# A hybrid decoder layer: gate tiles spread among the mixer's projections, a pool of their own for the first results of each feed-forward, and later places for two kinds of transposes

## The chip, the cores and the metric

The kernel runs on one core of a Trainium2 chip. TensorE multiplies matrices, VectorE, ScalarE and GpSimd (DVE, ACT and POOL in the profile) work on tiles in the on-chip memory SBUF and on the accumulators' banks in PSUM (GpSimd on SBUF alone here), and SyncE issues most of the transfers. The metric is the time of one execution on the device in microseconds, lower is better. Each engine works through its own list of instructions in order, and waits where an instruction needs something that is not there yet.

## The reference

One layer of a decoder for two groups of requests: 1024 tokens of one prompt, and 8 sequences of 4 new tokens each with a past of 4096. Width 1024, inner width of the feed-forward 2816, all in fp32:

```python
x += 1/2 * gate1 * SwiGLU1(mod(RMSNorm(x)))
x += gate2 * W_out [GDN heads | MLA heads](mod(RMSNorm(x)))
x += 1/2 * gate3 * SwiGLU2(mod(RMSNorm(x)))

def swiglu_ffn(h, wi, wo):
    gate, up = jnp.split(h @ wi, 2, axis=-1)
    return (jax.nn.silu(gate) * up) @ wo

def causal_conv(prev, x, w):
    xin = jnp.concatenate([prev.astype(x.dtype), x], axis=1)
    y = sum(xin[:, j:j + T] * w[j] for j in range(GDN_CONV))
    return jax.nn.silu(y), xin[:, xin.shape[1] - (GDN_CONV - 1):]
```

`mod` is a shift and a scale per sequence, worked out from a conditioning vector. The mixer's input projection has 2992 columns: 1536 for the queries, keys and values of 8 gated-delta heads (a convolution over 4 tokens and SiLU run over them, queries and keys are scaled to length 1 per head), 512 for the gate `z` of their output (SiLU), 16 for two small factors, 768 for the queries of 8 latent-attention heads, 128 for the latents, and 32 for rotary keys.

## The kernel before

The 1056 tokens lie as columns in 4 blocks of 264 (1024 channels as 8 groups of 128 rows). Every fp32 product is three matmuls of a rounded format, weights high by input high, high by low, low by high (`mm3`, lines 127 to 129), so inputs and weights are first split in a high part (ScalarE) and a low part (VectorE or GpSimd; `halve`, lines 369 and 370).

Stages by the trace: the start with the conditioning and the first norm up to about 50 us; the first feed-forward's up product to 575; its down product to 860; the mixer's projections 868 to 1283; the heads to 1974; the mixer's output to 2082; the second feed-forward's up product to 2550 and its down product to the end.

**Order.** The program is written as instructions with priorities, and a scheduler lists them per engine by priority and by when it expects their inputs; `high_priority(n)` moves what stands in it ahead by n, `later(n)` back by n. GpSimd's part is listed in the order of the program.

**Mixer's projections** (`mixer_in`, line 1259). `ORDER` (line 44) names the column tiles of 128 in their order: k, q, v (convolved), m (latent queries), c (latents), z (gate), and two marks, I (the inverses of the 64 x 64 triangular blocks, 31 steps at lines 1082 and 1084, all on VectorE) and F (the finish of the latent queries, nine token tiles on lines 1106 to 1166). A tile is 4 groups of 24 matmuls into a bank `pp`, one per block. After each group `hook` lets the follow-up work of earlier tiles go one step on; that work is written as generators. A convolved tile then costs: copies out of the bank (ScalarE), one tap on ScalarE and three on VectorE (line 913), SiLU (915, 916), nine transposes back to tokens (`to_tokens`, bank `ptk`, line 701), for queries and keys the sum of squares (930) and the scaling (938) of `tok`, and the way back to channels as eight transposes (`channels`, bank `pch`, line 953), twice. Values are scaled from ptk (1050, 1053). A gate tile costs one SiLU per group, straight out of its bank (`zt`, line 1246), and a store: nothing on VectorE or GpSimd. `raw`, `cy`, `tok` and `zt` are tiles of small rings. Three groups of transposes (`pnc`, line 1336) at the end collect the new state of the convolution.

**Feed-forward up** (`ffn_up`, line 505). Per tile of 128 inner columns there are seven products of 12 matmuls (`PRODUCTS`) for each pair of blocks, into three banks X, Z, Y. `ffn_pair` reads them: `s1` copies X to SBUF (line 487), `u2`, `u3` and the halves of `cc` add banks to it on VectorE (line 476), `sg` is SiLU, and `cc` is stored. In the first and the last tile the two pairs go one after the other, else in turn. The input of a pair, tiles B and T (sums and differences of the normed blocks, split in halves), is made by VectorE and ScalarE (lines 354 to 405, 369, 370) just ahead of the first tile, per block from `rb`, the reciprocal root mean square of every token broadcast over the rows (line 347). `norm_sums` (line 326) works it out from `nacc`.

**Mixer's output** (`mixer_out`, line 2079) works through eight output tiles, the last two for blocks 2 and 3 at the end, while blocks 0 and 1 are already normed for the second feed-forward. `LATE` holds the numbers that put the small matmuls of these norms later; its fourth is the one for `rb` of block 2.

## Time and profile before

| | us |
|---|---|
| three runs | 2831.9, 2836.54, 2845.81 (median 2836.54) |
| the profiled execution | 2833.71 |
| its span on the core | 2830.8 |
| TensorE busy in the span | 2659.3 (94%) |
| VectorE busy | 1716.5 (61%) |
| ScalarE / GpSimd busy | 1082.2 / 1082.9 (38% each) |
| mean granted clock of TensorE | 0.956 |

The span is from the first to the last instruction on the core; the execution lasts 2.9 us longer. "Idle before" is the time that an engine waited ahead of an instruction, followed by what ended the wait. A matmul's end is modelled, and they overlap, so the spacing of their starts is the surer number. PEclk is the clock that was granted to TensorE, as a share of the full one.

### The profile page before, as it was taken

How to read it: one execution, taken by the hardware profiler on the slowest of the kernel's cores; microseconds unless marked ns; L12 is line 12 of the kernel's file. 1: busy time of each engine (PE TensorE's matmuls, PEld its weight loads, DVE VectorE, ACT ScalarE, POOL GpSimd, SP SyncE). 2: the span in 40 equal slices, each digit the busy share in tenths (PEclk: the TensorE clock that was granted, in tenths of full speed). 3: DMA queues.
4: the chain of work that ended last, by engine and by line, in shares of the span. 5: the costliest groups of instructions: out<-in, count | busy, mean ns of one | idle time of the engine just before them, and what ended most of it. 6: DMA issues, size and time to landing. Idle time of an engine off the chain costs nothing.

```text
span 2830.8 us, 53341 instructions
## 1 busy us (share of the span) xinstructions
PE 2659.3 (94%) x21536; PEld 2459.8 (87%) x21536; DVE 1716.5 (61%) x3315; ACT 1082.2 (38%) x2055; POOL 1082.9 (38%) x1032
## 2 busy tenths in 40 slices
PE   4899999989999898799999999998979999999999
PEld 3788989989998887788888877776979999999999
DVE  7644444555564678856766666875585554546555
ACT  5322223322134543424666665553443333331111
POOL 0222223223342555653444465671433333323331
PEclk7999999999999899898999999997979999999999
DMA  7454452243232473432112243323422222234322
GB/s 274 149 172 128 128 165 91 72 173 99 85 102 78 150 205 115 146 130 83 44 51 62 61 97 107 103 66 95 147 73 91 76 84 76 84 111 140 99 76 70
DMA packets 339489, 308.34 MB, mean 109 GB/s; under 512 B 93865, under 2 KB 282017, under 8 KB 336171
## 3 DMA queue, kind: packets, MB, share of 16 engines
q1 hardware_dynamic: 304837, 246.32, 28.5%
q10 hardware_dynamic: 28262, 37.64, 4.1%
q0 software_dynamic: 6144, 20.98, 2.3%
q8 instruction: 169, 2.77, 0.4%
q14 instruction: 77, 0.63, 0.1%
HBM read 229.29 MB, written 75.59 MB: 108 GB/s over the span
## 4 chain that ended last, share of the span: by engine, by line
PE 43%; DVE 5%; issue 3%; POOL 3%; DMA 2%; ACT 1%; POOLq 0%; DVEq 0%; ACTq 0%; SPq 0%
PE po L127 4%; PE po L128 4%; PE po L129 4%; PE pY L127 2%; PE pY L128 2%; PE pY L129 2%; PE kraw L127 2%; PE pX L127 2%; PE pX L128 2%; PE pX L129 2%; PE pZ L127 1%; PE pZ L129 1%; PE kraw L128 1%; PE pZ L128 1%; PE kraw L129 1%
## 5 line engine op out<-in xcount | busy, mean ns | idle before, releaser
L127 PE MATMUL po<-act,whi 128*128 128x264 f32 x1408 | 403.5, 287 | 8.9 <-DVE x L435 5.3
L129 PE MATMUL po<-act,wlo 128*128 128x264 f32 x1408 | 402.9, 286 | 0.0
L128 PE MATMUL po<-act,whi 128*128 128x264 f32 x1408 | 401.3, 285 | 0.0
L435 DVE SCALAR_TENSOR_TENSOR x<-po,modT,x 128x264 f32<-128x264 f32 (+1 forms) x416 | 195.6, 481 | 240.7 <-PE po L129 240.1
L127 PEld LDWEIGHTS po<-act,whi 128*128 128x128 f32 x1408 | 266.8, 189 | 10.0 <-DVE x L435 5.9
L129 PEld LDWEIGHTS po<-act,wlo 128*128 128x128 f32 x1408 | 266.4, 189 | 0.0
L128 PEld LDWEIGHTS po<-act,whi 128*128 128x128 f32 x1408 | 266.3, 189 | 0.0
L370 POOL TENSOR_TENSOR A<-wg,A 128x512 fp32r<-128x512 f32 x84 | 110.9, 1321 | 372.4 <-ACT A L369 371.5
L2019 DVE TENSOR_REDUCE kss<-ksq 128x8 f32<-128x512 f32 x256 | 173.1, 682 | 101.8 <-ACT ksq L2018 100.1
L127 PE MATMUL pp<-hhi,whi 128*128 128x264 f32 (+1 forms) x768 | 226.1, 295 | 4.5 <-DVE nt L354 3.6
L128 PE MATMUL pp<-hlo,whi 128*128 128x264 f32 (+1 forms) x768 | 225.2, 293 | 0.0
L129 PE MATMUL pp<-hhi,wlo 128*128 128x264 f32 (+1 forms) x768 | 223.4, 292 | 0.0
L111 POOL TENSOR_TENSOR wlo<-wraw,whi 128x1024 fp32r<-128x1024 f32 x39 | 97.7, 2511 | 313.7 <-ACT whi L108 313.7
L127 PE MATMUL pX<-B,A 128*128 128x264 f32 x704 | 204.0, 290 | 10.6 <-ACT B L369 9.7
L128 PE MATMUL pX<-B,A 128*128 128x264 f32 x704 | 203.0, 288 | 8.9 <-DVE B L370 8.9
L2018 ACT ACTIVATE ksq<-kraw 128x512 f32<-128x512 f32 x256 | 152.2, 598 | 135.6 <-PE kraw L129 121.4
L128 PE MATMUL pY<-T,S 128*128 128x264 f32 x704 | 200.7, 285 | 2.1 <-DVE T L370 2.1
L129 PE MATMUL pX<-B,A 128*128 128x264 f32 x704 | 201.8, 287 | 0.0
L129 PE MATMUL pY<-T,S 128*128 128x264 f32 x704 | 200.2, 284 | 0.0
L127 PE MATMUL pY<-T,S 128*128 128x264 f32 x704 | 200.2, 285 | 0.0
L1718 POOL TENSOR_TENSOR plo<-pf,phi 128x512 fp32r<-128x512 f32 (+1 forms) x96 | 96.8, 1015 | 184.2 <-ACT phi L1717 169.7
L108 ACT CAST whi<-wraw 128x1024 fp32r<-128x1024 f32 x60 | 61.9, 1047 | 262.4 <-PE po L128 241.0
(539 smaller groups left out, 8238.4 us busy)
## 6 DMA issues: line engine op xcount, KB each, us to landing
adaw<-ada_w SPq DMA_DIRECT2D x72, 512.0 KB
wraw<-ffn_wi SPq DMA_DIRECT2D x46, 512.0 KB
act_d<-cc SPq DMA_DIRECT2D x88, 264.0 KB
wraw<-ffn_wo SPq DMA_DIRECT2D x44, 512.0 KB
wg<-ffn_wi SPq DMA_DIRECT2D x42, 512.0 KB
araw<-act_d ACTq DMA_DIRECT2D x160, 132.0 KB
x_d<-x SPq DMA_DIRECT2D x12, 1056.0 KB
wraw<-w_in SPq DMA_DIRECT2D x23, 512.0 KB
```

Source lines behind the costliest of these rows:

```text
L108: nc.scalar.copy(hi, raw)
L111: eng.tensor_tensor(out=lo, in0=raw, in1=f(hi), op=ALU.subtract)
L127: nc.tensor.matmul(out, whi, ahi, start=first, stop=False, **kw)
L128: nc.tensor.matmul(out, whi, alo, start=False, stop=False, **kw)
L129: nc.tensor.matmul(out, wlo, ahi, start=False, stop=last, **kw)
L370: eng.tensor_tensor(out=lo, in0=src, in1=f(hi), op=ALU.subtract)
L435: nc.vector.scalar_tensor_tensor(out=x[:, d, :n], in0=ps[:, :n], scalar=self.modT[:, m, d, 0:1], in1=x[:, d, :n], op0=ALU.mult, op1=ALU.add)
L1718: nc.gpsimd.tensor_tensor(out=lo[:, off:], in0=pf[:, off:], in1=f(hi[:, off:]), op=ALU.subtract)
L2018: nc.scalar.activation(sq, kr, AF.Square)
L2019: nc.vector.tensor_reduce(out=ss[:, (j * 4 + m) * H:(j * 4 + m + 1) * H], in_=sq.rearrange("p (h d) -> p h d", h=H), axis=AX.X, op=ALU.add)
```

## The change

It has five parts.

1. `ORDER` puts z0, z1 and z2 between the latent-query, query and value tiles, keeps z3 at the end, starts the inverses one tile earlier, puts q0 ahead of m4, and lays v0 between q2 and q3.
2. The transposes ptk and pch get a priority that is lower by `BEHIND` = 120.
3. The first inner tile of the first pair of blocks has `s1` (and `u2` in the same place), `u3` and half of `cc` in a small pool of its own, `early`, which is there from the start of the stage; before, they lie in memory that the stage ahead has to give back. Its product with `sg` is split in halves for that, and its seven products get a priority that is higher by `SOON` = 300. The other tiles are asked for in the reverse order for that pair.
4. The root of the mean square gets `SOON` too, `nacc` has two buffers in place of four, and `rb` of block 2 is put later by 12 and not 30.
5. In the mixer's output the last tile of weights lies in the slot `lo1` and its low half is made by VectorE and not by GpSimd; the first weights of the second feed-forward are loaded ahead of the last two output products.

Numbers of instructions stay the same on TensorE, ScalarE and SyncE; VectorE has three more and GpSimd one less.

The end of the projections on TensorE, where the heads begin (pp: projection; here z3; pqg, pwk and pqk are the heads' first products). Before, and then with the change:

```order
L127 MATMUL pp<-hhi_9313,whi 128x264
L128 MATMUL pp<-hlo_9314,whi 128x264
L129 MATMUL pp<-hhi_9313,wlo 128x264
L1773 MATMUL pqg<-ident,qg 96x32 x8
L1781 MATMUL pwk<-ident,wukf 64x128 x8
L1623 MATMUL pqk<-ident,mtok 96x128 x8
L1786 MATMUL pqa<-qsTt,wukTt 128x32 x4
```

```order
L131 MATMUL pp<-hlo_9319,whi 128x264
L132 MATMUL pp<-hhi_9318,wlo 128x264
L716 MATMUL ptk<-ident,raw 128x128 x6
L716 MATMUL ptk<-ident,raw 32x128
L1352 MATMUL pnc<-ident,ncv 27x128 x4
L716 MATMUL ptk<-ident,raw 128x128 x2
L1352 MATMUL pnc<-ident,ncv 27x128 x4
L1789 MATMUL pqg<-ident,qg 96x32 x8
L1797 MATMUL pwk<-ident,wukf 64x128 x8
L1639 MATMUL pqk<-ident,mtok 96x128 x8
```

The transposes of v3 and those that collect the state now stand between the last projection and the heads; before, they stood among the gate tiles.

The transposes of k0 among the projections, with tile numbers: first before (pp_10562 is the second block's group of the next tile), then with the change (pp_10672 is the group after it, of the third block):

```order
L129 MATMUL pp_10562<-hhi1_9024,wlo_9970 128x264
L127 MATMUL pp_10562<-hhi1_9024,whi_9969 128x264
L128 MATMUL pp_10562<-hlo1_9025,whi_9969 128x264
L701 MATMUL ptk_10268<-ident_58,raw_9369 128x128 x4
L701 MATMUL ptk_10277<-ident_58,raw_9369 128x128 x4
L701 MATMUL ptk_10286<-ident_58,raw_9369 32x128
L129 MATMUL pp_10562<-hhi1_9024,wlo_9970 128x264
```

```order
L130 MATMUL pp_10672<-hhi2_9238,whi_9974 128x264
L131 MATMUL pp_10672<-hlo2_9239,whi_9974 128x264
L716 MATMUL ptk_10273<-ident_58,raw_9374 128x128 x3
L716 MATMUL ptk_10282<-ident_58,raw_9374 128x128
L716 MATMUL ptk_10273<-ident_58,raw_9374 128x128
L716 MATMUL ptk_10282<-ident_58,raw_9374 128x128 x2
L716 MATMUL ptk_10291<-ident_58,raw_9374 32x128
L716 MATMUL ptk_10282<-ident_58,raw_9374 128x128
```

They stand some 40 matmuls later, and the single transposes of the three banks are mixed with each other.

VectorE at the start of the second feed-forward (st: norm of block 2; nv, nr, nq: the root; B: the second pair's input; s, u, c: the first pair's results). Before, and with the change:

```order
L319 TENSOR_TENSOR nacc<-nacc,nsq 128x264
L354 TENSOR_TENSOR st<-x_22689,rb 128x1056 x2
L336 TENSOR_SCALAR nv<-ss 66x4
L359 TENSOR_SCALAR st<-st,modT 128x264 x4
L707 TENSOR_SCALAR nr<-nv 66x4
L713 TENSOR_TENSOR nq<-nr 66x4
L714 SCALAR_TENSOR_TENSOR nq<-nq,nv 66x4
L715 SCALAR_TENSOR_TENSOR nr<-nq,nr 66x4
L370 TENSOR_TENSOR B_23836<-st,B_23836 128x1056
L713 TENSOR_TENSOR nq<-nr 66x4
L370 TENSOR_TENSOR B_23839<-st,B_23839 128x1056
```

```order
L481 TENSOR_TENSOR u_24078<-s_24037,pZ 128x264
L358 TENSOR_TENSOR st<-x_22697,rb 128x1056 x2
L340 TENSOR_SCALAR nv<-ss 66x4
L481 TENSOR_TENSOR c_24023<-u_24078,pY 128x264
L363 TENSOR_SCALAR st<-st,modT 128x264
L722 TENSOR_SCALAR nr<-nv 66x4
L363 TENSOR_SCALAR st<-st,modT 128x264 x3
L728 TENSOR_TENSOR nq<-nr 66x4
L729 SCALAR_TENSOR_TENSOR nq<-nq,nv 66x4
L481 TENSOR_TENSOR u_24078<-s_24037,pY 128x264
L730 SCALAR_TENSOR_TENSOR nr<-nq,nr 66x4
L374 TENSOR_TENSOR B_23872<-st,B_23872 128x1056
```

Four additions of the first pair (one just ahead of the piece) now stand ahead of the halves of the second pair's input; before, none. On TensorE, the matmuls of the first pair that stand ahead of rb of block 2 there are 48, before 29.

The diff:

```diff
--- before.py
+++ after.py
@@ -41,7 +41,7 @@
             ("T1", "S1", "Y", False), ("T4", "A22", "Z", True), ("B22", "S4", "Y", True))
 
 
-ORDER = "k0 k1 m0 m1 k2 k3 c0 m2 I0 m3 m4 m5 F0 q0 q1 q2 q3 v0 v1 v2 v3 z0 z1 z2 z3"
+ORDER = "k0 k1 m0 m1 k2 k3 c0 I0 m2 m3 q0 m4 m5 z0 F0 q1 z1 q2 v0 q3 z2 v1 v2 v3 z3"
 
 PSQ = 3
 WENG = 1
@@ -65,7 +65,10 @@
 AHEAD = 1500
 
 
-LATE = (100, 150, 110, 30, 110)
+LATE = (100, 150, 110, 12, 110)
+SOON = 300
+
+BEHIND = 120
 
 
 def f(ap):
@@ -311,7 +314,7 @@
             sq = tp.tile([P, 2, BW], F32, tag="nsq", name="nsq", bufs=2)
             nc.scalar.activation(sq[:, :m], x[:, k:k + m, :], AF.Square)
             if k == 0:
-                self.nacc[b] = acc = tp.tile([P, BW], F32, tag="nacc", name="nacc", bufs=NB)
+                self.nacc[b] = acc = tp.tile([P, BW], F32, tag="nacc", name="nacc", bufs=2)
                 eng.tensor_tensor(out=acc, in0=sq[:, 0], in1=sq[:, 1], op=ALU.add)
             else:
                 acc = self.nacc[b]
@@ -333,8 +336,9 @@
                 for q in range(4):
                     nc.tensor.matmul(ss[:W, 4 * at + q:4 * at + q + 1], self.nacc[b][:, q * W:(q + 1) * W], self.ones, start=True, stop=True)
         v, r, t = (tp.tile([W, 4 * NB], F32, tag=n, name=n, bufs=3)[:, 0:n_] for n, n_ in (("nv", n), ("nr", n), ("nq", n)))
-        nc.vector.tensor_scalar(v, ss[:W, 0:n], 1.0 / D, EPS, ALU.mult, ALU.add)
-        self.rsqrt(r, v, t)
+        with self.tc.high_priority(SOON):
+            nc.vector.tensor_scalar(v, ss[:W, 0:n], 1.0 / D, EPS, ALU.mult, ALU.add)
+            self.rsqrt(r, v, t)
         for at, b in enumerate(blocks):
             self.nr[b] = r[:, 4 * at:4 * at + 4]
 
@@ -469,12 +473,15 @@
         part("S4", A12, nc.vector)
         return W
 
-    def ffn_pair(self, p, W, dst, tp, ps, products):
+    def ffn_pair(self, p, W, dst, tp, ps, products, early=None):
+
 
         nc = self.nc
         T = lambda n: tp.tile([P, self.ffn_tiles[n][0]], F32, tag=f"{n}{p}", name=n, bufs=self.ffn_tiles[n][1])
         tt = lambda out, a, b, op=ALU.add: nc.vector.tensor_tensor(out=out, in0=a, in1=b, op=op)
         sg, cc = T("sg"), T("cc")
+        E = lambda n: early.tile([P, BW], F32, name=n) if early else T(n)
+        c1 = E("c1") if early else cc[:, BW:]
         B, F = {}, self.forms[p]
         for x, w, bank, add in products:
             if not add:
@@ -483,41 +490,48 @@
                 self.mm3(B[bank], W[w][:, 0, k], W[w][:, 1, k], F[x][:, 0, k], F[x][:, 1, k], k == 0 and not add, k == 3 and (add or x == "T2"),
                          skip_group_check=True)
             if x == "B11":
-                s1 = T("s1")
+                s1 = E("s1")
                 nc.scalar.copy(s1, B["X"])
             elif x == "T2":
-                u2, u3 = T("u2"), T("u3")
+                u2, u3 = s1 if early else T("u2"), E("u3")
                 tt(u2, s1, B["Y"])
                 tt(u3, u2, B["Z"])
             elif x == "B21":
                 nc.scalar.activation(sg[:, :BW], B["X"], AF.Silu)
             elif x == "T1":
-                tt(cc[:, BW:], u3, B["Y"])
+                tt(c1, u3, B["Y"])
             elif x == "T4":
                 tt(cc[:, :BW], u2, B["Z"])
             elif x == "B22":
                 tt(u3, u2, B["Y"])
                 nc.scalar.activation(sg[:, BW:], u3, AF.Silu)
-                tt(cc, sg, cc, ALU.mult)
+                if early:
+                    tt(cc[:, BW:], sg[:, BW:], c1, ALU.mult)
+                    tt(cc[:, :BW], sg[:, :BW], cc[:, :BW], ALU.mult)
+                else:
+                    tt(cc, sg, cc, ALU.mult)
                 nc.sync.dma_start(out=dst[:, 2 * BW * p:2 * BW * p + 2 * BW], in_=cc)
             yield
 
-    def ffn_up(self, wi, tp, ps, hook=lambda us: None, first=None):
+    def ffn_up(self, wi, tp, ps, hook=lambda us: None, first=None, early=None):
 
 
         nf = wi.shape[1] // 2 // P
+
 
         self.ffn_tiles = {"cc": (2 * BW, 2), "sg": (2 * BW, 1), "u3": (BW, 1), "u2": (BW, 1), "s1": (BW, 1)}
         for p in range(2):
-            for n, (w, bufs) in self.ffn_tiles.items():
+            for n, (w, bufs) in list(self.ffn_tiles.items())[::1 if p else -1]:
                 tp.tile([P, w], F32, tag=f"{n}{p}", name=n, bufs=bufs)
         for ff in range(nf):
             W = first if first and ff == 0 else self.ffn_weights(wi, ff, tp)
             order = PRODUCTS if ff else (PRODUCTS[0], PRODUCTS[3], *PRODUCTS[1:3], *PRODUCTS[4:])
-            pairs = [self.ffn_pair(p, W, self.act_d[ff], tp, ps, order) for p in range(2)]
+            pairs = [self.ffn_pair(p, W, self.act_d[ff], tp, ps, order, early if ff + p == 0 else None) for p in range(2)]
             for g in pairs if ff in (0, nf - 1) else [zip(*pairs)]:
-                for _ in g:
-                    hook(1.45 if g in pairs else 2.9)
+
+                with self.tc.high_priority(SOON if ff == 0 and g is pairs[0] else 0):
+                    for _ in g:
+                        hook(1.45 if g in pairs else 2.9)
 
     def ffn_down(self, wo, mgate, tp, ap, ps, each, load):
 
@@ -696,9 +710,10 @@
         nc = self.nc
         for t0, n, sz in ((0, 4, P), (4, 4, P), (8, 1, NS)):
             pt = ps.tile([P, 4, P], F32, tag="B", name="ptk")
-            for t in range(n):
-                c0 = (t0 + t) * P
-                nc.tensor.transpose(pt[:sz, t, :m], row[:m, c0:c0 + sz], self.ident[:m, :m])
+            with self.later(BEHIND):
+                for t in range(n):
+                    c0 = (t0 + t) * P
+                    nc.tensor.transpose(pt[:sz, t, :m], row[:m, c0:c0 + sz], self.ident[:m, :m])
             sink(t0, n, sz, pt)
 
     def rsqrt(self, y, v, t):
@@ -949,8 +964,9 @@
         nc = self.nc
         for g in range(2):
             pt = ps.tile([P, 512], F32, tag="B", name="pch")
-            for t in range(4):
-                nc.tensor.transpose(pt[:, t * P:(t + 1) * P], tok[:, 4 * g + t].rearrange("p r d -> p (r d)"), self.ident)
+            with self.later(BEHIND):
+                for t in range(4):
+                    nc.tensor.transpose(pt[:, t * P:(t + 1) * P], tok[:, 4 * g + t].rearrange("p r d -> p (r d)"), self.ident)
             nc.scalar.copy(out[:, 512 * g:512 * (g + 1)], pt)
 
     def pair_products(self, lT, rT, dm, ps):
@@ -2076,7 +2092,7 @@
                     for _ in smp:
                         pass
 
-    def mixer_out(self, tp, tn, ps, then):
+    def mixer_out(self, tp, tn, ps, then, ahead):
 
 
         nc, wo = self.nc, self.i["w_out"][0]
@@ -2101,7 +2117,12 @@
             if h == 0:
                 self.norm_sums(pair, tn, ps)
                 side = then(0, then(1, iter(())))
-        ws = [load(d) for d in range(KT - 2, KT)]
+
+        ws = [load(KT - 2)]
+        raw, t = self.load_cols(wo, (KT - 1) * P, P), self.slot("lo1", [P, KT * BW], F32R, "wlast")
+        ws.append([t[:, n * D:n * D + D].rearrange("p (k c) -> p k c", k=KT) for n in range(2)])
+        self.halve(*ws[1], raw, nc.vector)
+        ahead()
         for b in pair:
             for n, w in enumerate(ws):
                 product(b, KT - 2 + n, w)
@@ -2153,7 +2174,7 @@
         k.setup()
         k.dram()
         with k.weights():
-            with k.extra():
+            with k.extra(), pool("tf") as early:
                 with k.residents(), ExitStack() as pse, pool("tn") as tn, pool("t0") as tp:
                     ps = banks(pse, "ps0", **DOWN)
                     k.small_vectors(ps, "C")
@@ -2187,7 +2208,7 @@
                         while credit[0] > 0:
                             next(bg, None)
                             credit[0] -= PACE
-                    k.ffn_up(ins["ffn1_wi"][0], tp, ps, hook, first)
+                    k.ffn_up(ins["ffn1_wi"][0], tp, ps, hook, first, early)
                     run(bg)
             with k.residents(), ExitStack() as pse, pool("a1", side="right") as a0, pool("b1", side="right") as a1, pool("tn1") as tn:
                 ps = banks(pse, "ps2", **DOWN)
@@ -2222,7 +2243,7 @@
         with heads:
             k.mixer_heads()
         with k.weights():
-            with k.extra():
+            with k.extra(), pool("tf2") as early:
                 with k.residents(), ExitStack() as pse, pool("tn2") as tn:
                     ps = banks(pse, "ps3", **DOWN)
                     k.load_xb(k.x1_d, nc.sync)
@@ -2234,9 +2255,10 @@
                         k.store_xb(k.x2_d, b)
                         if not b:
                             yield from side
-                    k.mixer_out(tn, tn, ps, then)
+                    ready = []
+                    k.mixer_out(tn, tn, ps, then, lambda: ready.append(k.ffn_weights(ins["ffn2_wi"][0], 0, None)))
                 with ExitStack() as pse, pool("t2") as tp:
-                    k.ffn_up(ins["ffn2_wi"][0], tp, banks(pse, "ps4", **UP))
+                    k.ffn_up(ins["ffn2_wi"][0], tp, banks(pse, "ps4", **UP), first=ready[0], early=early)
             with k.residents(), ExitStack() as pse, pool("a2", side="right") as a0, pool("b2", side="right") as a1, pool("tn3") as tn:
                 ps = banks(pse, "ps5", **DOWN)
```

## The prediction

> **What bounds the kernel now.** I read the page first: the busy time of the engines, then the span in 40 slices, to see where TensorE, which carries nearly all of the work, is not busy.
>
> ```profile
> span 2830.8 us, 53341 instructions
> PE 2659.3 (94%) x21536; PEld 2459.8 (87%) x21536; DVE 1716.5 (61%) x3315; ACT 1082.2 (38%) x2055; POOL 1082.9 (38%) x1032
> PE   4899999989999898799999999998979999999999
> DVE  7644444555564678856766666875585554546555
> PEclk7999999999999899898999999997979999999999
> ```
>
> TensorE is busy for 2659.3 of 2830.8 us, so 171.5 us of idle time is the most that reordering can win outright. The idle time is in few places: slices 1 and 2 (the start), 15 to 17 (one slice is 70.8 us, so 1062 to 1274 us: the mixer's projections), and 29 to 31 (the mixer's output and the start of the second feed-forward). The change touches all three. So the second view is busy time by stretch, for just those. Columns: stretch, length, then PE, PEld, DVE, ACT and POOL busy, the granted clock, DMA share and GB/s.
>
> ```profile
> 40.00:84.60 44.60, 17.60 (x91) 15.23 (x89) 44.51 (x53) 29.56 (x45) 5.81 (x5) 0.62 0.32 120
> 984.50:1064.50 80.00, 75.78 (x625) 71.25 (x626) 62.10 (x187) 33.12 (x73) 43.26 (x67) 0.97 0.77 212
> 1064.50:1251.00 186.50, 151.12 (x1275) 144.70 (x1272) 154.90 (x357) 67.05 (x144) 114.18 (x146) 0.86 0.38 129
> 1251.00:1282.60 31.60, 31.60 (x263) 31.48 (x260) 3.06 (x7) 4.31 (x11) 3.05 (x5) 1.00 0.30 95
> 1282.60:1300.00 17.40, 12.93 (x93) 11.58 (x93) 8.95 (x27) 4.42 (x7) 10.38 (x11) 0.72 0.73 226
> 2070.00:2108.00 38.00, 19.28 (x108) 17.75 (x107) 31.25 (x61) 17.23 (x28) 4.86 (x5) 0.66 0.23 85
> ```
>
> From 1064.5 to 1251 us (the query and value tiles) VectorE is 83% busy and TensorE idle for 35.4 us; from 1251 to 1282.6 (gate tiles) TensorE is full and VectorE has 3.06 us to do. One engine waits for the other, and then the other way round. The waits of TensorE from 1064.5 to 1282.6 say what ends its idle time (us in total, times, longest), and its timeline shows two of the four long ones:
>
> ```profile
> PE pch L953 <- DVE tok L938: 21.3, 4, 5.9
> PE pch L953 <- POOL cy L101: 6.7, 5, 2.4
> PE ptk L701 <- ACT raw L916: 3.3, 1, 3.3
> PE ptk L701 <- ACT raw L915: 3.1, 3, 1.5
> PE pk L965 <- DVE hs L715: 1.0, 1, 1.0
> 1085.05 1.03 PE L701 MATMUL ptk<-ident,raw 128*128 128x128 f32 x8
> 1103.14 1.97 PE L953 MATMUL pch<-ident,tok 128*128 128x128 f32 x8 [5.44 <-DVE tok L938]
> 1188.08 1.94 PE L953 MATMUL pch<-ident,tok 128*128 128x128 f32 x8 [4.18 <-DVE tok L938]
> ```
>
> The waits sum to 35.4 us, the whole idle time. In each query tile the way back to channels (pch, line 953) stands on TensorE ahead of projection work, and tok, which it reads, comes late from VectorE: 18.1 us after the first ptk (1103.14 less 1085.05).
>
> **The change part by part.**
>
> *Gate tiles spread out.* Price of a gate tile: the projection matmuls alone (tile pp), in the same columns without POOL.
>
> ```profile
> 1064.50:1251.00 186.50, 118.30 (x868) 115.05 (x868) 0.00 (x0) 12.47 (x43) 0.86 0.38 129
> 1251.00:1282.60 31.60, 31.57 (x260) 31.48 (x260) 0.00 (x0) 4.31 (x11) 1.00 0.30 95
> ```
>
> In the full stretch a matmul takes 31.57/260 = 0.1214 us, a tile of 96 takes 11.7 us. Three of the four tiles leave the end: 3 x 11.7 = 35.0 us of work without any VectorE, laid where TensorE waits. In the stretch with waits a matmul takes 118.30/868 = 0.1363 us at a clock of 0.86; without the waits the 868 would take 105.4 us, 12.9 us less. So TensorE's own work from 984.5 to 1282.6 us (298.1 us) is 75.8 + 151.1 + 31.6 - 12.9 = 245.6 us, and VectorE's is 62.1 + 154.9 + 3.1 = 220.1 us. If they overlapped fully, the stage would end 52 us sooner; if VectorE's chain grew longer by what it waits for, by nothing.
>
> Between the two I go by stretches of the new order. The groups of VectorE's work from 1064.5 to 1251 us (columns: count, busy us, mean ns, idle before) and the block inverse's two lines from 984.5 to 1251 us:
>
> ```profile
> L913 DVE SCALAR_TENSOR_TENSOR cy<-raw,convw,cy 128x1080 f32<-128x1080 f32 x24 | 37.3, 1555 | 0.2
> L938 DVE TENSOR_TENSOR tok<-tok,trs 128x1024 f32<-128x1024 f32 x4 | 5.3, 1316 | 0.0
> L930 DVE TENSOR_REDUCE tss<-tsq 128x8 f32<-128x512 f32 x8 | 5.4, 677 | 1.7 <-ACT tsq L929 1.6
> L1050 DVE TENSOR_TENSOR cy<-ptk,beta 128x256 f32<-128x256 f32 x16 | 5.8, 414 | 0.3 <-PE ptk L701 0.2
> L1053 DVE COPY cy<-ptk 32x128 f32<-32x128 f32 x4 | 1.1, 274 | 4.9 <-PE ptk L701 4.9
> L1166 DVE TENSOR_TENSOR mq<-mq,hs 128x512 f32<-128x512 f32 x9 | 7.0, 781 | 0.1
> L1161 DVE TENSOR_REDUCE hs<-mqs 128x8 f32<-128x512 f32 x9 | 6.1, 680 | 6.4 <-ACT mqs L1158 6.4
> L1082 DVE TENSOR_TENSOR inv<-M 128x62 f32<-128x62 f32 (+15 forms) x31 | 21.8, 703 | 0.3
> L1084 DVE TENSOR_TENSOR M<-M,inv 128x62 f32<-128x62 f32 (+15 forms) x31 | 23.2, 749 | 0.5
> ```
>
> The inverse is 45.0 us. A value tile is three taps (3 x 1.555) and four scalings (4 x 0.414) and a little: 6.6 us, three of them 20 us. Six tiles stand in each of two new stretches (m2 m3 q0 m4 m5 z0, then q1 z1 q2 v0 q3 z2) and four in the last (v1 v2 v3 z3). TensorE has 70 us of projections in each of the first two and 47 in the last; I estimate its transposes and small products (245.6 less 16 x 11.7, so 59 us) at 29, 19 and 6 by where their tiles stand, the rest ahead: 99, 89, 53. For VectorE the last has three value tiles and the rest of the latent queries, about 27 us. Of the 193 us left, the middle one, with three query tiles and most of the latent queries, takes somewhat more than half, about 108, the first about 85 to 92. The longer engine in each: 99, 108 and 53 or so, 260 us in sum, which is 38 us less than now; with no more than a third of the present waits left (12 us) it is 26 less. I take the middle of these, **-32 us**, between 0 and -52.
>
> *What stands at the end now.* Before, the gate tiles covered the last value tile; now its transposes stand behind the last projection, with the heads' first products behind them. The last stretch of the table, 1282.6 to 1300, has 4.5 us of idle TensorE already. Eight transposes cost 1.03 us (ptk above, of the same shape), the four scalings 1.7, one turn to copy the state about as much: **+4 us**, between 0 (it hides behind the heads' loads) and +9 (a wait as long as the long ones above, 5.9, and the transposes on top).
>
> *Transposes behind.* The same counts of instructions; they stand some 40 to 60 projection matmuls later (5 to 7 us at 0.1214). Where TensorE was waiting for a transpose's input (3.3 + 3.1 us at ptk, 28 us at pch), this turns a wait into work. Where VectorE was the one that waits, its next step is late by these 5 to 7 us. I take **0**: the gain is already in the 32. Ends: -6.4 (all of the ptk waits) and +8 (one delay of the whole chain).
>
> *Early pool, first feed-forward.* The first tile's results of the first pair no longer wait for memory of the stage before, so four products (48 matmuls, 5.8 us at 0.1214) can run while the second pair's input is being made:
>
> ```profile
> 62.39 0.59 PE L127 MATMUL pX<-B,A 128*128 128x264 f32 x1 [4.47 <-ACT B L369]
> 73.78 0.59 PE L127 MATMUL pZ<-T,S 128*128 128x264 f32 x1 [4.54 <-ACT T L369]
> 84.64 0.39 PE L127 MATMUL pX<-B,A 128*128 128x264 f32 x1 [0.94 <-ACT s L487]
> ```
>
> But VectorE is busy for 44.51 of these 44.60 us, so each of the additions that now go ahead (0.43 us each, below) lengthens that bound: seven are 3.0 us. **-2 us**, between -5.8 and +3.0.
>
> *Early pool, second feed-forward.* Here TensorE waits for the second pair's input three times:
>
> ```profile
> 2084.60 2.42 DVE L354 TENSOR_TENSOR st<-x,rb 128x1056 f32<-128x1056 f32 x2 [2.55 <-PE rb L347]
> 2089.14 0.59 PE L127 MATMUL pX<-B,A 128*128 128x264 f32 x1 [3.20 <-ACT B L369]
> 2101.83 0.59 PE L127 MATMUL pZ<-T,S 128*128 128x264 f32 x1 [8.17 <-ACT T L369]
> 2109.02 0.43 DVE L476 TENSOR_TENSOR u<-u,pZ 128x264 f32<-128x264 f32 x1
> ```
>
> The 48 matmuls would fill 5.8 us. But rb, which opens that input's chain, now stands behind 48 matmuls of the first pair and not 29: 19 more, 2.3 us; and four additions stand ahead on VectorE, 1.7 us. **-1.5 us**, between -5.8 and +4. The last output tile's weights, halved by VectorE and no longer by POOL, one operation, and the second feed-forward's first weights, loaded two products earlier, lie beside full products: 0, with the cover gone the one operation, below 1.3 us by L938 of nearly the same width.
>
> **Sum:** -32 + 4 + 0 - 2 - 1.5 = -31.5 us on this execution, 2833.7 us with what lies around its span; 2802. The median of the three runs, 2836.5, is 2.8 above it, so **2805 us**.
>
> [...]
>
> **The rivals.**
>
> *VectorE is the bound (2832).* It has 220.1 us to do in 298.1, and 83% in the waiting stretch. For it: 21.3 of the 35.4 us of waits are for VectorE's tok, and its chain of a query tile is serial. If the chain stretches by as much as gate work is put between its steps, the 35 us move from the end into the middle and what remains is 2836.5 + 4 - 3.5 and -5, most of the 6.7 us that pch waits for POOL: 2832. Against: VectorE sat idle for 28.5 us beside the gate tiles, and the inverse (45 us, without TensorE) now starts a tile earlier.
>
> *Late transposes starve VectorE (2857).* Each of the 12 convolution tiles' ptk stands behind projections instead of ahead; VectorE's next step (L1050, L930) waits for it. It loses when VectorE has less than 5 to 7 us of other work queued, and then in every tile of the VectorE-bound part: seven tiles (q and v but the last) at 6 us are 42, and with 10 more for the key tiles ahead, 2805 + 52 = 2857. Against: L1050 and L1053 wait 0.3 and 4.9 us for ptk in all, so there is mostly work queued now.
>
> [...]
>
> *The early pool does nothing at the second feed-forward* would cost 1.5 us against the forecast and decides no sign.
>
> **How the numbers follow.** Forecast, some 20 to 40 us gained: 0.55. Full fit: 0.17. VectorE the bound: 0.15. Starved: 0.13. The range for eight in ten cuts half of the starved case and the edge of the full fit: 2782 to 2834; the likeliest case's own range is 2793 to 2818. A difference under 0.5%, 14 us, is what a measurement of this kernel can't tell from none. Faster, below 2822: forecast and full fit, 0.72. Within: 0.15. Slower, above 2851: half or more of the starved case, and what I can't name, 0.13.
>
> **What would show it.** Right: the waits of pch for tok fall from 21.3 us to under 10; the granted clock in the query part rises from 0.86 over 0.93; the projections' last matmul comes 25 to 35 us before 1282.6; the four transposes of the last value tile cost under 6 us ahead of the heads; at 2070 to 2108 no more than two of these waits shrink. Wrong: ptk appears as what ends VectorE's waits, with over 10 us; or the waits move from pch to an equal sum elsewhere; or a stage that the change doesn't touch is longer.

## The result, and the profile after

The changed kernel takes 2814.34 us (median of 6 runs, 2807.92 to 2823.72), the one before 2840.35 us beside it (6 runs). The ratio is 0.9908, with a 95% interval of 0.9882 to 0.9935: some 26 us faster, 19 to 34. Forecast were 2805 us and a gain of 31.5; the time lies in the stated range (2782 to 2834). The profiled execution took 2812.38 us. Its page:

```profile
span 2810.6 us, 53194 instructions
PE 2657.6 (95%) x21536; PEld 2456.7 (87%) x21536; DVE 1672.2 (59%) x3318; ACT 1078.3 (38%) x2055; POOL 1073.9 (38%) x1031
PE   5999999999999899799999999998979999999999
DVE  7644444465574679866667656785584445455555
PEclk7999999999999899898999998996989999999999
```

Slices 2, 9 and 16 of TensorE are at nine tenths or more now; the holes at 14, 17, 28 and 30 are still there. So I cut both spans at the same events: the first matmul of pX, of the down product's po, of the projections' pp, the last pp, the first psn of the heads, the first po of the mixer's output, the first and last po of the second down product. (Cut so, the first down product ends at 847.5 us before the change and the projections begin at 847.6, not at 860 and 868; at 868 they go on after a wait of 3.6 us.) Busy time in three of these stretches (columns as in the prediction), first before, then after: the first down product with the passage into it, the projections, and the heads' start up to psn.

```profile
578.00:847.60 269.60, 262.55 (x2146) 262.01 (x2145) 158.07 (x330) 60.89 (x74) 96.68 (x54) 0.99 0.32 103
847.60:1282.40 434.80, 382.45 (x3222) 364.64 (x3221) 299.65 (x727) 172.64 (x360) 214.90 (x293) 0.92 0.44 135
1282.60:1296.50 13.90, 9.43 (x59) 8.40 (x59) 8.01 (x23) 4.42 (x7) 7.77 (x8) 0.77 0.66 205
```

```profile
574.10:837.10 263.00, 260.32 (x2147) 259.53 (x2146) 156.91 (x334) 62.07 (x76) 96.45 (x53) 1.00 0.34 113
837.10:1260.50 423.40, 373.16 (x3205) 357.33 (x3203) 297.73 (x716) 172.63 (x360) 198.94 (x291) 0.93 0.43 133
1260.50:1282.70 22.20, 14.43 (x78) 12.03 (x77) 13.24 (x35) 4.62 (x7) 11.55 (x11) 0.65 0.78 244
```

The projections, for which 32 us were forecast, became 11.4 us shorter (434.8 to 423.4), and the heads' start 8.1 us longer (14.1 to 22.2, from the last pp). The mixer's part together gave 3.3 us. The first down product, where nothing was forecast, gave 6.6 us. The total came near the forecast, but from other places. The waits of TensorE from 837 to 1300 us after the change (engine and line waited for, us in total, times, longest):

```profile
PE pch L969 <- DVE tok L953: 24.4, 6, 11.2
PE ptk L716 <- ACT raw L930: 6.5, 3, 2.6
PE ptk L716 <- ACT raw L931: 6.1, 1, 6.1
PE pqg L1789 <- DVE qg L1785: 4.6, 1, 4.6
...
PE pqk L1639 <- DMA mtok<-qc_d: 3.0, 1, 3.0
```

The wait of pch for tok, 21.3 us before, didn't shrink: it is 24.4 us, with one wait of 11.2 us in it, and two waits at the heads' start are new (pqg, pqk).

All kernels by stage, in us, from one profiled execution each; the ratio and its interval are from the timed runs against the kernel before.

| kernel | up 1 | down 1 | projections | heads' start | heads | out + up 2 | down 2 | ratio (95%) |
|---|---|---|---|---|---|---|---|---|
| before | 528.4 | 269.6 | 434.8 | 14.1 | 678.5 | 578.3 | 270.2 | 1 |
| the change | 524.5 | 263.0 | 423.4 | 22.2 | 680.4 | 573.8 | 266.4 | 0.9908 (0.9882 to 0.9935) |
| e1 order alone | 526.8 | 269.1 | 420.2 | 18.1 | 679.2 | 579.7 | 268.9 | 0.9952 (0.9939 to 0.9966) |
| e2 order and later transposes | 531.2 | 268.4 | 421.9 | 20.7 | 676.4 | 574.7 | 275.1 | 0.9986 (0.9972 to 1.0) |
| e3 block of offset 0 alone | 530.5 | 262.5 | 436.4 | 14.4 | 684.7 | 577.4 | 269.4 | 0.9981 (0.9968 to 0.9995) |
| e4 change without that block | 524.7 | 267.7 | 426.0 | 19.8 | 679.6 | 573.4 | 268.7 | 0.9951 (0.9932 to 0.997) |
| e5 change, transposes not later | 523.6 | 262.3 | 417.3 | 16.6 | 682.5 | 571.5 | 266.7 | 0.9878 (0.9859 to 0.9898) |
| e6 e5, z2 at the end | 523.4 | 263.3 | 419.9 | 6.8 | 673.4 | 571.0 | 267.0 | 0.9831 (0.9812 to 0.9849) |
| e7 e5, latent queries later | 523.1 | 262.4 | 414.3 | 21.9 | 684.5 | 572.8 | 266.6 | 0.9892 (0.9875 to 0.9908) |
| e8 e5, queries' pch later | 523.0 | 263.3 | 417.3 | 17.9 | 678.8 | 572.1 | 266.6 | 0.9888 (0.9872 to 0.9905) |
| e9 change without early pool | 527.8 | 262.7 | 425.4 | 22.1 | 679.0 | 575.9 | 269.3 | 0.9953 (0.9938 to 0.9967) |
| e10 e6 with later transposes | 523.0 | 262.7 | 427.9 | 20.3 | 680.8 | 570.8 | 266.4 | 0.9884 (0.986 to 0.9907) |
| e11 e6, z1 at the end too | 525.2 | 263.0 | 430.8 | 14.5 | 682.8 | 572.8 | 266.5 | 0.9918 (0.9899 to 0.9938) |
| e12 e6, latent queries later | 524.2 | 262.6 | 415.6 | 20.0 | 684.4 | 572.7 | 266.5 | 0.9894 (0.9871 to 0.9917) |

A single stage scatters: the heads, which no edit touches beyond a few rows' order, range from 673.4 to 684.7 us. I read stage differences under 3 us as nothing, and of the long stages under 5.

### The profile page after: what moved, and what is told of

Same layout as the page of the kernel before. It is cut to its first block, busy times and chain, and to the rows that moved or that the text cites. A ratio compares the mean times of both kernels' runs of the same rounds, so it can differ in the third digit from the quotient of the medians.

```text
span 2810.6 us, 53194 instructions
## 1 busy us (share of the span) xinstructions
PE 2657.6 (95%) x21536; PEld 2456.7 (87%) x21536; DVE 1672.2 (59%) x3318; ACT 1078.3 (38%) x2055; POOL 1073.9 (38%) x1031
## 4 chain that ended last, share of the span: by engine, by line
PE 76%; DVE 10%; DMA 5%; issue 3%; POOL 3%; ACT 2%; SPq 0%; ACTq 0%; DVEq 0%; POOLq 0%
PE po L130 7%; PE po L132 7%; PE po L131 7%; PE pY L130 4%; PE pY L131 4%; PE pY L132 4%; PE pX L131 3%; PE pX L130 3%; PE pZ L130 3%; PE pZ L131 3%; PE pX L132 3%; PE pZ L132 3%; PE kraw L130 2%; PE pp L130 2%; PE kraw L132 2%
## 5 line engine op out<-in xcount | busy, mean ns | idle before, releaser
L481 DVE TENSOR_TENSOR cc<-u,pY 128x264 f32<-128x264 f32 x86 | 36.7, 426 | 211.8 <-PE pY L132 207.8
```

The source lines that it names most:

```text
L481: tt = lambda out, a, b, op=ALU.add: nc.vector.tensor_tensor(out=out, in0=a, in1=b, op=op)
```

## The experiments

### Order and transposes apart (e1, e2)

```diff
-ORDER = "... m2 I0 m3 m4 m5 F0 q0 q1 q2 q3 v0 v1 v2 v3 z0 z1 z2 z3"
+ORDER = "... I0 m2 m3 q0 m4 m5 z0 F0 q1 z1 q2 v0 q3 z2 v1 v2 v3 z3"
 # e2 beside this, ptk and pch:
+            with self.later(BEHIND):
```

> The kernel before with the new order of column tiles alone; transposes and feed-forwards as before. Compared by stage: from the first projection of the mixer to the first psn product of the heads (before 448.9 us, with the whole change 445.6). Theory A (as predicted: the gate tiles fill TensorE's waits, worth 20 to 40 us less some 4 at the heads' start): 410 to 432 us here too, and the whole change got less only because the late transposes took it back. Theory B (read from the two traces: the query tiles' scaling waits in VectorE's queue between the steps of the latent queries, so waits move and stay): 440 to 450 us, total within 8 us of before. The feed-forwards stay within 3 us of before by both.

> The kernel before with the new order and the later transposes, the whole mixer part of the change, feed-forwards as before. First projection to first psn: 445.6 us as with the whole change, by both theories (within 4). Theory A: at least 10 us longer than with the order alone (late transposes take the gain). Theory B: within 5 us of the order alone, or shorter; total some 0 to 8 us below before, so that most of the 26 us of the whole change is elsewhere.

Measured: 2823.12 and 2832.65 us, against 2837.08. The order alone gained 14 us, and the later transposes took 10 of them back, 4 to 15 by the two intervals. From the first pp to psn e1 has 438.3 us, e2 442.6. The 438.3 lie between the two theories (410 to 432 by A, 440 to 450 by B), nearer to B. On the transposes the two readings differ: the total shows the 10 us of theory A, but the stretch for which both theories were stated shows 4.3, which is what B allowed. The rest of the difference lies in stages that the edit doesn't touch, and those scatter by up to 6.2 us between these two executions. The busy time and the waits of e1's projections:

```profile
845.80:1266.00 420.20, 371.14 (x3218) 355.28 (x3217) 301.06 (x723) 172.64 (x360) 201.99 (x291) 0.95 0.44 135
PE pch L953 <- DVE tok L938: 14.8, 4, 7.7
PE ptk L701 <- ACT raw L915: 9.1, 3, 5.1
PE ptk L701 <- DVE dml L966: 5.0, 1, 5.0
PE ptk L701 <- ACT raw L916: 4.6, 1, 4.6
```

Of the 14.6 us by which the projections became shorter, 11.3 are TensorE's busy time (382.45 to 371.14 for nearly the same matmuls, at a granted clock of 0.95 and not 0.92), and only 3.3 are idle time (52.35 to 49.06). The waits for tok fell by 6.5 us, and new ones came at ptk: it waits for VectorE's work on pair products (dml) and for ScalarE's SiLU. Tile by tile, the first pch of the query tiles q1 and q2 before (those of q0 and q3 stand in the prediction, with 5.44 and 4.18 us), then of q0 to q3 in e1:

```profile
1132.18 1.94 PE L953 MATMUL pch<-ident,tok 128*128 128x128 f32 x8 [5.91 <-DVE tok L938]
1159.98 1.94 PE L953 MATMUL pch<-ident,tok 128*128 128x128 f32 x8 [5.76 <-DVE tok L938]
```

```profile
1078.76 1.46 PE L953 MATMUL pch<-ident,tok 128*128 128x128 f32 x8 [4.54 <-DVE tok L938]
1140.20 1.03 PE L953 MATMUL pch<-ident,tok 128*128 128x128 f32 x8
1185.56 1.94 PE L953 MATMUL pch<-ident,tok 128*128 128x128 f32 x8 [7.68 <-DVE tok L938]
1220.30 1.06 PE L953 MATMUL pch<-ident,tok 128*128 128x128 f32 x8 [2.38 <-DVE tok L938]
```

Between a query tile's first ptk and its first pch stand 95, 51, 30 and 34 projection matmuls before (q0 to q3, counted in the trace), and 33, 100, 41 and 96 in e1. In q1 and q3, where more stand between now, the wait is gone or smaller; in q0 it fell by under 1 us, and in q2 it grew.

### The block of offset 0 (e3, e4)

The change puts the loop over a tile's products in a block whose offset is 300 for one pair and 0 for all the others:

```diff
 # e3, on the kernel before
+                with self.tc.high_priority(0):
                     for _ in g:
                         hook(1.45 if g in pairs else 2.9)
 # e4, on the change
-                with self.tc.high_priority(SOON if ff == 0 and g is pairs[0] else 0):
+                with self.tc.high_priority(SOON) if ff == 0 and g is pairs[0] else nullcontext():
```

> The kernel before with one edit: the products of every inner tile of both feed-forwards stand in a high_priority block of offset 0, as all but the first pair's do in the change. Offset 0 asks for nothing, but what is in such a block doesn't advance the counter of priorities, so every inner tile and the down product behind them begin at the same number. Theory C (this is where the unforecast 6.6 and 3.8 us at the passages from up to down product come from): the stretch from the first po product to the first projection falls from 269.6 to 263 to 265 us, the second one from 270.3 to 266 to 268, the total by 8 to 14 us, without any early pool. Rival D (the early pool and the reverse order of the tiles' places do it, the block of offset 0 is nothing): both stretches within 2 us of before, total within 4 us.

> The changed kernel, with the block of high priority kept for the first pair of the first inner tile alone and no block of offset 0 around the others. Theory C: the passages from up to down product go back to 269 to 270 us each (263.0 and 266.5 with the change), total 2822 to 2828 us. Rival D: no difference, 2814 us and both stretches within 2 us of the change.

Measured: 2832.66 us (ratio 0.9981, 1 to 9 us less than before) and 2821.28 us (ratio 0.9951 against 0.9908 with the block). Alone it brings the first passage with its down product from 269.6 to 262.5 us; taken out, that goes back to 267.7, and the second from 266.4 to 268.7. So theory C holds at the first passage on both sides, though e3's total fell by less than the 8 to 14 us that it named; at the second passage neither e3 (269.4 against 270.2) nor e4 (2.3 us) shows more than is read as nothing. What differs at the first passage is VectorE's list. Before, a product with sg waits for ScalarE, with the evacuation of po behind it; after, the evacuations start 4.6 us after the first po (578.68 less 574.1) and not 9.3 (587.34 less 578.0):

```profile
582.24 1.23 DVE L111 TENSOR_TENSOR wlo<-wraw,whi 128x1024 fp32r<-128x1024 f32 x1 [3.60 <-ACT whi L108]
586.72 0.71 DVE L476 TENSOR_TENSOR cc<-sg,cc 128x528 f32<-128x528 f32 x1 [3.25 <-ACT sg L500]
587.34 2.89 DVE L435 SCALAR_TENSOR_TENSOR x<-po,modT,x 128x264 f32<-128x264 f32 x7
```

```profile
578.68 0.48 DVE L439 SCALAR_TENSOR_TENSOR x<-po,modT,x 128x264 f32<-128x264 f32 x1
579.08 0.70 DVE L481 TENSOR_TENSOR cc<-sg,cc 128x528 f32<-128x528 f32 x1
579.70 2.48 DVE L439 SCALAR_TENSOR_TENSOR x<-po,modT,x 128x264 f32<-128x264 f32 x6
```

The two runs bear this out: the evacuations start 4.6 us after the first po in e3 (585.07 less 580.5) and 8.8 us after it in e4 (583.54 less 574.7). TensorE's wait for them in the first 40 us of the passage follows; before, then e3:

```profile
PE po L127 <- DVE x L435: 5.3, 1, 5.3
```

```profile
PE po L127 <- DVE x L435: 0.8, 1, 0.8
```

With the change it is 0.8 us too, and 4.9 in e4. So this wait is 4 to 4.5 of the 5 to 7 us.

### The change without the later transposes (e5)

```diff
-            with self.later(BEHIND):
```

> The changed kernel with the two kinds of transposes where they were (no lower priority), all else as changed. From the first pair of runs: the new order alone gained 13.7 us, with the later transposes 4.1 us. If the later transposes cost these 9.6 us here too (theory A, VectorE is starved): 2803 to 2808 us, and the stretch from the first projection to the first psn 436 to 440 us (445.6 with the change). Rival: in the whole change their cost is no more than the 4.3 us that the stages showed (442.6 against 438.3 us), the rest being other stages' scatter: 2808 to 2812 us.

Measured: 2802.8 us, ratio 0.9878 against 0.9908: 8.5 us by the ratios, 11.5 by the medians. The two intervals overlap, so that this pair alone doesn't settle it; e1 with e2 above (10 us) and e6 with e10 below (18 us) point the same way. By stages it is 6.1 us in the projections and 5.6 at the heads' start. In the projections of e5 pch waits 14.0 us for tok, as in e1 (14.8), and not 24.4. What VectorE waits for shows where the loss begins. Its wait for the transposes of the tile of the small factors (tb), with the change and then in e5:

```profile
DVE tb L805 <- PE ptk L716: 11.8, 1, 11.8
```

```profile
DVE tb L804 <- PE ptk L715: 3.0, 1, 3.0
```

It is 11.8 us in all five kernels with the later transposes (the change, e2, e4, e9, e10) and 3.0 in all nine without. The loss follows soon: when 768 of the 2304 projection matmuls have been started, about where the key tiles are worked off, the change is 5.7 us behind e5, and at the end 6.1; e2 is 4.8 behind e1 there and 1.7 at the end, e10 6.3 behind e6 and 8.0. So the loss in the projections is that of a VectorE kept waiting early, and the longer waits for tok in the query tiles add little to it. Wait and loss go together in all three pairs; no run moved tb's transposes alone.

### What the query tiles wait for (e7, e8)

```diff
 # e7, on e5
-ORDER = "... z0 F0 q1 z1 q2 v0 q3 z2 v1 v2 v3 z3"
+ORDER = "... z0 q1 z1 q2 F0 q3 v0 z2 v1 v2 v3 z3"
 # e8, on e5: in gdn_q, ahead of channels
-        yield from self.wait(LAG[2])
+        yield from self.wait(3)
```

> As e5, with the finish of the latent queries begun after q2 and not after z0. Theory B (the scaling of a query tile is late because its small steps stand in VectorE's list among those of the latent queries): waits of pch for tok in the projections fall from some 20 to 25 us to under 12 us, the projections end 5 to 12 us sooner than e5 unless the finish runs into the heads. Rival (VectorE is the bound over the whole stretch, in whatever order): the waits move behind q3, projections and heads' start together within 3 us of e5.

> As e5, with the way back to channels of a query tile (pch) put two steps later, 48 projection matmuls or 5.8 us, in TensorE's list; pk and the stores follow it. If TensorE's waits for tok are only a matter of where pch stands, 4 waits of 4 to 6 us turn into work: the projections end 10 to 18 us sooner than e5, waits of pch for tok under 6 us in all. If VectorE is the bound, the waits appear at ptk or at the heads' start and the total is within 4 us of e5.

Measured: 2807.57 and 2806.09 us; neither is better than e5 (2802.8). In e7 (which puts v0 behind q3 too) the waits for tok fall from 14.0 to 9.0 us and the projections take 3.0 us less, so that the latent queries' steps in VectorE's list seem to play a part; but the heads' start grows from 16.6 to 21.9, and the gain is gone, as the rival said. e8 is the clearer of the two. Its waits of TensorE from 837 to 1285 us:

```profile
PE ptk L715 <- DVE dml L980: 8.5, 1, 8.5
PE ptk L715 <- ACT raw L930: 7.5, 2, 4.5
PE pqg L1787 <- DVE qg L1783: 6.4, 1, 6.4
PE ptk L715 <- ACT raw L929: 6.1, 4, 2.1
...
PE pk L979 <- DMA kT<-kT_d: 3.3, 1, 3.3
...
PE pch L967 <- DVE tok L952: 1.9, 2, 1.7
```

The wait for tok is gone (14.0 to 1.9 us), and the projections take 417.3 us as in e5. The waits moved to the next product of VectorE (dml, 4.8 to 8.5 us), to ScalarE's SiLU (at ptk 11.4 to 13.6 us), and to a transfer. The place of pch in TensorE's list isn't what bounds this stage. That leaves the pace of the follow-up work, on VectorE and ScalarE; no run made that work shorter, so this is argued and not shown.

### Which tiles stand at the end (e6, e10, e11, e12)

```diff
 # e6, on e5
-ORDER = "... q1 z1 q2 v0 q3 z2 v1 v2 v3 z3"
+ORDER = "... q1 z1 q2 v0 q3 v1 v2 v3 z2 z3"
 # e10: e6 with the later transposes.  e11: "... q1 q2 v0 q3 v1 v2 v3 z1 z2 z3"
 # e12: "... z0 q1 z1 q2 F0 q3 v0 v1 v2 v3 z2 z3"
```

> As e5, but z2 moved from between q3 and v1 to the end, so that two gate tiles cover the last value tile. The heads' start (last projection to first psn: 14.1 us before, 22.2 with the change, 18.1 with the order alone) is 14 to 16 us if it is the uncovered transposes and state rows of v3 that lengthen it; the projections then lose up to 4 us of fill (z2 took waits of q3 and v1) and the total lies within 3 us of e5. If z2 filled full waits where it was, 6 to 12 us are lost there and the total is above e5.

> e6 (two gate tiles at the end) with the later transposes again: the changed kernel but for the place of z2. The later transposes cost 11.5 us in the changed kernel (2814.3 against 2802.8 us). If they cost it because v3's transposes end up behind the last projection with nothing to cover them, little is left here, since two gate tiles follow: within 4 us of e6, 2786 to 2793 us. If VectorE is starved in every convolved tile (the prediction's rival), 6 to 14 us are lost here too: 2795 to 2803 us, with the waits at the key tiles (5 us more in the changed kernel than before).

> e6 with z1 moved to the end too: three gate tiles there and one in the middle. If what counts is only that the heads' start is covered, one tile more at the end covers nothing new and z1's 11.7 us of fill are lost in part: 4 to 10 us above e6, heads' start still about 7 us. If VectorE's share of the heads' start is again held up by the gate tiles' memory, as before the change (14.1 us with four at the end), the heads' start grows to 10 to 14 us.

> e6 with the latent queries' finish after q2 as in e7. There the projections ended 3 us sooner but the heads' start took 21.9 us, since VectorE still had the finish to do. With two gate tiles as cover, theory: projections 415 to 418 us and heads' start 7 to 10 us, total within 4 us of e6 (2785 to 2793 us). If the finish doesn't fit under the two tiles (27 steps, of which 20 stand beside q3 and the value tiles), the heads' start is 12 to 20 us and the total 2795 us or more.

Measured: e6 2788.82 us, 14 less than e5 (6 to 21 by the intervals), more than the 3 expected; e10 2806.86, e11 2814.21, e12 2805.67, all three as slow as the worse case stated for them or slower. (e12 differs from e6 in the place of v0 too.) In e10 the later transposes cost 8.0 us in the projections, with two gate tiles as cover: that part is not the uncovered end but VectorE fed late, by the rows of tb above. A further 13.5 us are at the heads' start. e6 is the fastest kernel here, 0.9831 (0.9812 to 0.9849) of the one before. Its projections are 2.6 us longer than e5's, within what is read as nothing, and its heads' start is 6.8 us and not 16.6. So the two stages explain 7.2 us of the gain. Its heads, 673.4 us, are 9.1 us under e5's, more than is read as nothing, and no run says why; the profiled execution is the quickest of its four. The other three have two or three gate tiles at the end too, and don't get it. VectorE's first steps of the heads point to a reason. Rows of before, then of e6, of e10 and of e11:

```profile
1274.41 0.69 DVE L1766 TENSOR_TENSOR wukf<-wukh,wukl 128x512 f32<-128x512 f32 x1 [19.36 <-ACT zt L1246]
1286.04 0.48 DVE L1793 MEMSET zero<- 128x512 f32 x1 [10.14 <-DMA z_d<-zt]
```

```profile
1245.98 0.67 DVE L1780 TENSOR_TENSOR wukf<-wukh,wukl 128x512 f32<-128x512 f32 x1
1248.81 0.48 DVE L1807 MEMSET zero<- 128x512 f32 x1 [1.36 <-DMA new_conv_sample<-ncvo]
```

```profile
1270.58 0.69 DVE L1782 TENSOR_TENSOR wukf<-wukh,wukl 128x512 f32<-128x512 f32 x1 [11.94 <-DMA z_d<-zt]
```

```profile
1272.59 0.48 DVE L1807 MEMSET zero<- 128x512 f32 x1 [15.55 <-DMA z_d<-zt]
```

wukf and zero read nothing of a gate tile, yet wait for one to be made or stored. They are the heads' first tiles, and I take it that they lie where a gate tile lay. Before, in e10 and in e11 that holds VectorE until after the last projection. In e6 neither waits for it, both are done at 1249.3 us, 7 us ahead of the end of the projections (1256.5), and TensorE goes from the projections to the heads without a wait. The same 60 or so matmuls then take 6.8 us; before they took 9.6 us of busy time at a granted clock of 0.77, with 4.5 us of waiting between them. (Behind that wait four matmuls of pqk take 1.09 us, and the same four in e6 0.64.) In the change and in e5 (one gate tile at the end) wukf is late mainly for the reason that was forecast: v3's scalings and state rows stand ahead of it. (A wait for a store, of 1.6 and 1.9 us, comes on top.) In e12 it runs at 1260.95 us, directly behind the latent queries' last steps on VectorE, 8 us after the last projection. Which ring slot the last gate tiles take, and so which of the heads' tiles waits for them, depends on the order as a whole; no run moved that slot alone, so this last step is read from the waits and not shown by an edit of its own.

### The early pool (e9)

```diff
-            ... self.ffn_pair(p, W, self.act_d[ff], tp, ps, order, early if ff + p == 0 else None)
+            ... self.ffn_pair(p, W, self.act_d[ff], tp, ps, order, None)
```

> The changed kernel without the early pool: the first pair's first results lie in the stage's own memory as before (its higher priority, the reverse order of places and all other parts stay). By the prediction the pool is worth 2 us at the first feed-forward and up to 1.5 at the second, so 2816 to 2819 us, and the stretches up1 (first pX to first po, 524.5 us with the change, 528.4 before) and out+up2 (first mixer output product to the second down product, 573.8 with the change, 578.3 before) are 1 to 4 us longer each. If the pool gives nothing and the block of offset 0 and the moved norms give it all, both are within 1 us of the change.

Measured: 2821.67 us, ratio 0.9953 (0.9938 to 0.9967) against 0.9908; the first up product takes 3.3 us longer, output and second up product 2.1. Both sizes are those expected, the second under what is read as nothing. The total is over the 2816 to 2819 us expected, and the ratios say 13 us, with 4 to 21 by the intervals; the stages don't say where the rest is. The second down product has 2.9 us of it (269.3 against 266.4), with the block of offset 0 in place.

## Why the prediction was right, and where it was wrong

The time, the sign and the likeliest case's own range (2793 to 2818) were right. The sum came out right by luck, since errors of its terms cancelled: the gate tiles gave 17 us less than forecast and the later transposes took about 10, while the feed-forwards gave some 15 us more than forecast, 10 of them in the down products, where no term stood.

**Gate tiles, -32 us: wrong in size.** Measured 14.6 us (e1), within the stated 0 to 52. The step that failed is "the longer engine in each", with "no more than a third of the present waits left (12 us)". It treats TensorE's waits as a pool that any free work can fill. But the wait is between two points of one query tile, its ptk and its pch, and a projection fills it only if it stands between them: in e1 that came about in q1 and q3, not in q0 and q2, and new waits came at ptk (5.0 and 5.1 us). 49.06 us of idle time remained of 52.35. What did come is the other part of the bound, the clock: 12.9 us were counted for it, and busy time fell by 11.3 (382.45 to 371.14 us, the granted clock from 0.92 to 0.95).

**The heads' start, +4 us: right for the order alone** (18.1 against 14.1 in e1), 8.1 with the whole change, within the stated 9. But the 14.1 us were taken as the least that this start takes; e6 has 6.8. The row that said so was in the trace of before (19.36 us of VectorE's waiting for zt) and wasn't followed.

**Transposes behind, 0 us, -6.4 to +8: wrong.** 8.5 to 11.5 us slower (e5), 10 in e2. The rival named the right mechanism and had the wrong size and place (52 us, "in every tile of the VectorE-bound part"): the loss is 6.1 us in the projections, 5.7 of it by the time the key tiles are worked off, after VectorE waited 11.8 us and not 3.0 for tb, and 5.6 at the heads' start, where v3's transposes now come after the last projection. "The gain is already in the 32" was the wrong step: turning a wait into work moved the wait, as e8 shows (14.0 to 1.9 us for tok, 4.8 to 8.5 for dml).

**Early pool, -2 and -1.5 us: right in sign and, by stages, in size**: 3.3 and 2.1 (e9), the second too small to be told from scatter; the total of e9 says more (13 us, 4 to 21) and stays open.

**Not forecast at all: the block of offset 0.** 6.6 us at the first passage, of which e3 and e4 put 5 to 7 down to it. The prediction has no term for the block, and the list of the change's parts leaves it out: an offset of 0 was read as no edit, and its effect looked for in no stage. The lists of VectorE in the two passages differ, and would have shown it. The page of before showed the hole as well: TensorE's slice 9 (566 to 637 us) is at eight tenths, and the prediction's places of idle time pass over it. (They also give slices 16 and 17, 1062 to 1203 us, as 15 to 17 up to 1274.)

**The signs.** Of the signs that the prediction named, one of being wrong came true: ptk ends 20.2 us of VectorE's waits from 837 to 1300 us (8.1 before), over the 10 named. Signs of being right failed: the waits of pch for tok did not fall under 10 us. The granted clock of the query part, over 0.93 by the forecast, is 0.89 from 1064 to 1226 us. The last projection comes 21.9 us sooner and not 25 to 35, and 10.5 of these are from the stages ahead.

**The rivals.** "VectorE is the bound" was the nearest for the stage: e8 and e7 show that waits move and stay, though in e8's projections ScalarE ends as much of them as VectorE (20.6 and 19.4 us). It was wrong in that the clock's 11 us came all the same. "The full fit", with 0.17 of the chances and the lower end of the range, stands for 2785 us and an overlap that no run shows: the projections became at most 20.5 us shorter (434.8 to 414.3, e7), of the 52 that a full overlap would give. The one kernel that comes close to 2785 us is e6 with 2788.8, and it gets there with 419.9 us of projections, not by the fit.

## What to carry to other kernels

A hole in an engine's list was filled here only by work that stood between its two ends (e1: the wait of q1, 5.91 us, is gone, and that of q3 fell from 4.18 to 2.38); free work elsewhere helped little or not (q0 from 5.44 to 4.54, q2 from 5.76 to 7.68), and moving the waiting instruction back moved the wait to the next one (e8: 14.0 to 1.9 us for tok, 4.8 to 8.5 for dml). The passage between two stages deserves its own row in the sum: what the first instructions of the next stage wait for, free memory included, was worth 10 us between e5 and e6 and 13.5 between e6 and e10, about as much as all refilling (14.6). And an edit that looks like nothing, a priority block of offset 0, is looked up in the instruction lists before it is costed at nothing.

## What was unexpected of the hardware

Some 3220 matmuls of the projections took 382 us of busy time at a granted clock of 0.92 and 371 at 0.95 (e1), with only 3.3 us less of idle time: the clock gave more than three times what the waits themselves did. The rows of pch show it at single waits: eight transposes took 1.46 to 1.97 us behind waits of 4.2 to 7.7 us, and 1.03 to 1.06 behind none or one of 2.4.

A small operation of VectorE takes four times its usual time in some places (0.66 us and not 0.16). After the change, one line and shape within 3 us, and GpSimd's work beside the first:

```profile
1167.41 0.66 DVE L729 SCALAR_TENSOR_TENSOR hs<-hs 128x16 f32<-128x16 f32 x1
1169.98 0.16 DVE L729 SCALAR_TENSOR_TENSOR hs<-hs 128x16 f32<-128x16 f32 x1
```

```profile
1166.61 2.82 POOL L104 TENSOR_TENSOR X<-M,low 128x256 f32<-128x256 f32 x4
```

It takes 0.66 us while GpSimd works through pieces of 0.7 us, and 0.16 once it has stopped. In the whole trace of the change 44 operations of this kind and shape (hs, lines 729 and 730) have no GpSimd instruction beside them, and none takes over 0.18 us; of the ten that have one, nine take over 0.4. So in these rows the longer time goes with GpSimd's work beside it; no run took that work away, and the cause is not shown.
